# Both output projections of a two-layer encoder as seven products of halves, with weight sums built by adding DMAs

## The chip, the cores and the metric

The kernel runs on one core of a Trainium2 chip. The metric is the device time in microseconds of one execution. A difference is read from the median of several runs; the profile comes from one execution, whose time is given beside its span.

## The reference

A trunk of two encoder layers over 1024 tokens of width 1024, all float32. Each layer normalises, modulates by the conditioning vector, mixes tokens, and adds the mixer's output through an output projection and a gate:

```python
mod = c_act @ ada_w[layer] + ada_b[layer]
shift, scale, gate = jnp.split(mod, 3, axis=-1)
h = rms_norm(x, norm_w[layer]) * (1.0 + scale[:, None, :]) + shift[:, None, :]
...
return jnp.concatenate([oa, ob], axis=-1) @ w_out      # layer 0
...
return (oc * jax.nn.silu(gc)) @ w_out                  # layer 1
...
x = x + gate[:, None, :] * y
...
return rms_norm(x, final_norm)
```

Layer 0 mixes with two attention groups, layer 1 with windowed attention. Only the two products with `w_out` (1024 x 1024 each) and what surrounds them are changed.

## The kernel before

Everything is kept transposed: 128 partitions hold features, the free dimension holds tokens. A float32 matmul is made of three (`mm3`): each operand is split into a high part, rounded to the fast format, and a low part, the rest; high by high, high by low and low by high are added in PSUM. So each operand costs a cast and a subtraction ahead of its use. Tiles of 128 x 1024 come from one pool of 49 (`U`, `UR`), accumulators from eight PSUM banks of 128 x 512.

The kernel isn't issued as it is written. A recorder takes down every operation, a list scheduler gives each a start, and `emit` writes them out in that order; so all instructions carry the line of `emit` (L483 in the profile, L548 in the changed kernel), and groups are told apart by the names of tiles. On each engine instructions then run strictly in that order. Marks (`b703`, `("w", 3, 6)`, `("op", half, ft)`) name points in the program after which a load may be issued.

An output projection (`load_wo`, `load_oT`, `out_proj`) runs twice per layer, for tokens 0 to 511 and 512 to 1023. For each of eight output tiles `ft` and eight contraction steps `kc`, `mm3` multiplies a 128 x 128 block of weights (`wo0h`, `wo0l`; `wo1h`, `wo1l`) with 512 tokens of the mixer's output (`oTh`, `oTl`). In layer 1 the second half is done in two blocks of 256 tokens, so that the last block's end is short. DVE's scalar_tensor_tensor evacuates: residual plus gate column (`gcol`) times PSUM, in place in the residual (`xr`, `x1r`). Behind it ACT squares the new residual and POOL or DVE adds the squares (`sq`); when a half is complete, PE transposes the sums, DVE reduces them (`ss`), POOL takes the power (`r`), PE transposes `r` back, and the rows are normalised: in layer 0 for layer 1's input (`hT10`, `hT11`), in layer 1 for the output. `ada_at(("op", half, ft))` hangs the computation of layer 1's modulation columns (DVE operations on tiles `ada` and `adag`, four per place) on output tiles of layer 0's projection. Loads run on SP's queue; POOL's queue issues only sixteen small copies (`q<-qr_sp`).

## Time and profile before

| | |
|---|---|
| median of 3 runs | 1194.38 us (1193.34 to 1195.65) |
| profiled execution | 1192.36 us |
| its span, first to last instruction | 1190.6 us |
| mean granted TensorE clock | 0.995 |
| layer 0's projection, first and last start of a matmul with wo0h | 651.5 and 741.5 us |
| layer 1's, with wo1h | 1074.3 and 1179.9 us |

An engine's busy time is a union over the stretch; the chain of work that ended last is followed back from the last instruction, so an engine that fills the chain sets the end. A line group gives the busy time, the mean duration of one instruction, and the idle time in front with what ended it. Matmuls are pipelined: the duration of one is longer than the distance to the next, and only the distance is paid.

### The profile page before, as it was taken

Reading aid. Unit: us, or ns where it says so; the run is one execution under the profiler, and the core shown is the slowest. Engines: PE = TensorE matmul, PEld = TensorE weight load, DVE = VectorE, ACT = ScalarE, POOL = GpSimd, SP = SyncE. Lnnn points to the kernel's source line nnn. Section 1 sums busy time; section 2 is a strip of 40 time slices with the busy share of each in tenths; the row PEclk is TensorE's granted clock in tenths of the full one; section 3 lists DMA queues with packets and bytes.
Section 4 is the critical chain, followed back from the end, with each engine's and each line's share of the span. In section 5 each row is a group of like instructions: output and inputs, shape, how many; then the busy total and the mean of one; then the engine's idle time right before and its main releaser. Section 6 shows DMA issues by size and latency. Waiting matters only on the chain.

```text
span 1190.6 us, 17868 instructions
## 1 busy us (share of the span) xinstructions
PE 1161.9 (98%) x6320; PEld 982.7 (83%) x6320; DVE 904.8 (76%) x1693; ACT 657.1 (55%) x1371; POOL 581.1 (49%) x591
## 2 busy tenths in 40 slices
PE   8999999999999999999999999999999999999996
PEld 7898887878778778788778888988888888888896
DVE  7974678797777988888889984559886697788343
ACT  5653366566646867786868221328755545653212
POOL 1334496859456555453448324306456254467321
PEclk9999999999999999999999999999999999999999
DMA  9602212131112210101044664200012121055112
GB/s 370 246 1 79 99 40 72 54 124 36 51 62 89 89 53 19 36 18 36 2 160 164 246 243 159 72 1 19 19 54 74 36 88 54 18 198 178 68 72 71
DMA packets 33353, 106.18 MB, mean 89 GB/s; under 512 B 3696, under 2 KB 6256, under 8 KB 33264
## 3 DMA queue, kind: packets, MB, share of 16 engines
q1 hardware_dynamic: 32496, 102.96, 24.1%
q0 software_dynamic: 768, 2.10, 0.7%
q8 instruction: 49, 0.80, 0.3%
q14 instruction: 40, 0.33, 0.1%
HBM read 82.36 MB, written 22.68 MB: 88 GB/s over the span
## 4 chain that ended last, share of the span: by engine, by line
PE 84%; DVE 6%; ACT 4%; DMA 3%; issue 1%; POOL 1%; SPq 0%; POOLq 0%; DVEq 0%; ACTq 0%
PE psum L483 84%; DVE nm L483 2%; DMA ada<-in_ada_t 2%; DVE p L483 1%; DMA w2s<-in_w_c 1%; DMA w31s<-in_w_c 1%; ACT k L483 1%; ACT q L483 1%; ACT Pa L483 0%; DVE hla L483 0%; ACT p L483 0%; DVE hl L483 0%; DVE q L483 0%; DVE hlb L483 0%; POOL r L483 0%
## 5 line engine op out<-in xcount | busy, mean ns | idle before, releaser
L483 DVE TENSOR_REDUCE nm<-psum 128x1 f32<-128x1024 f32 x128 | 154.7, 1217 | 24.6 <-PE psum L483 23.0
L483 POOL TENSOR_SCALAR p<-p,dn 128x384 f32<-128x384 f32 (+1 forms) x128 | 74.1, 597 | 160.2 <-DVE dn L483 79.2
L483 DVE TENSOR_TENSOR hla<-psum,hla 128x512 fp32r<-128x512 f32 x128 | 84.3, 683 | 18.4 <-ACT hla L483 17.2
L483 PE MATMUL psum<-hla,VA 128*128 128x512 f32 x256 | 93.9, 425 | 3.7 <-DVE hla L483 3.5
L483 POOL TENSOR_SCALAR Pb<-Pb,rs 128x1024 f32<-128x1024 f32 x64 | 71.8, 1124 | 45.6 <-DVE rs L483 43.9
L483 ACT CAST hla<-psum 128x512 fp32r<-128x512 f32 x128 | 71.5, 597 | 40.3 <-PE psum L483 37.1
L483 PE MATMUL psum<-ident,Pa 128*128 128x128 f32 x512 | 91.6, 273 | 1.4 <-DVE q L483 0.8
L483 PE MATMUL psum<-hlb,VB 128*128 128x512 f32 x256 | 90.7, 427 | 2.1 <-DVE hlb L483 1.4
L483 POOL TENSOR_SCALAR Pa<-Pa,rs 128x1024 f32<-128x1024 f32 x64 | 73.6, 1154 | 39.2 <-DVE rs L483 37.0
L483 ACT ACTIVATE Pa<-psum,nm 128x1024 f32<-128x1024 f32 x64 | 71.7, 1121 | 35.7 <-DVE nm L483 31.5
L483 DVE TENSOR_TENSOR hlb<-psum,hlb 128x512 fp32r<-128x512 f32 x128 | 82.2, 683 | 7.7 <-ACT hlb L483 6.9
L483 ACT ACTIVATE Pb<-psum,nm 128x1024 f32<-128x1024 f32 x64 | 71.8, 1123 | 25.2 <-DVE nm L483 22.2
L483 PE MATMUL psum<-k,q 128*128 128x512 f32 x256 | 84.1, 399 | 0.2 <-ACT Pb L483 0.2
L483 DVE CUSTOM_DVE_ANT_0 p<-psum,bias,rows_g 128x384 f32<-128x384 f32 (+1 forms) x128 | 70.5, 578 | 12.8 <-PE psum L483 11.7
L483 PE MATMUL psum<-ident,Pb 128*128 128x128 f32 x512 | 79.4, 272 | 0.0
L483 ACT ACTIVATE p<-p,nm 128x384 f32<-128x384 f32 (+1 forms) x128 | 74.1, 585 | 7.1 <-DVE nm L483 7.1
L483 PEld LDWEIGHTS psum<-ident,Pa 128*128 128x128 f32 x512 | 64.3, 140 | 12.9 <-DVE gT L483 1.6
L483 ACT COPY ot<-psum 64x512 f32<-64x512 f32 x64 | 37.4, 584 | 67.5 <-PE psum L483 67.0
L483 ACT CAST hlb<-psum 128x512 fp32r<-128x512 f32 x128 | 68.9, 603 | 9.1 <-PE psum L483 7.8
L483 PEld LDWEIGHTS psum<-ident,Pb 128*128 128x128 f32 x512 | 63.1, 140 | 11.3
L483 POOL TENSOR_TENSOR sq<-sq,sq 128x256 f32<-128x256 f32 (+2 forms) x22 | 27.6, 1254 | 78.2 <-ACT sq L483 77.9
L483 PE MATMUL psum<-oTl,wo1h 128*128 128x256 f32 (+1 forms) x192 | 61.1, 319 | 0.0
(750 smaller groups left out, 3647.5 us busy)
## 6 DMA issues: line engine op xcount, KB each, us to landing
ada<-in_ada_t SPq DMA_DIRECT2D x32, 512.0 KB, 8.6
adag<-in_ada_t SPq DMA_DIRECT2D x16, 512.0 KB, 4.9
o<-spill SPq DMA_DIRECT2D x12, 512.0 KB, 5.6
xT<-in_xt SPq DMA_DIRECT2D x8, 512.0 KB, 8.2
wo0s<-in_w_out SPq DMA_DIRECT2D x8, 512.0 KB, 8.1
xr<-in_xt SPq DMA_DIRECT2D x8, 512.0 KB, 10.8
x_sp<-xr SPq DMA_DIRECT2D x8, 512.0 KB, 3.0
wo1s<-in_w_out SPq DMA_DIRECT2D x8, 512.0 KB, 5.7
```

The lines of the kernel that those rows point to most:

```text
L483: fn(*[real(v) for v in a], **{k: real(v) for k, v in kw.items()})
```

## The change

`wino_out` takes the place of `load_oT`, `load_wo`, `out_proj` and the layers' loops, in both layers. Weights and activations are cut into 2 x 2 halves (A11 to A22 by halves of the output and of the contraction features, B11 to B22 by halves of the contraction features and tokens). Instead of eight half products, seven are formed, in the order of phases "1", "2", "6", "7", "4", "5", "3". Each has four output tiles `u`, four steps `k` and three matmuls, with 512 tokens; phase 3 of layer 1 is done in two blocks of 256.

- Sums of weights: S1 = A21 + A22, S2 = A11 + A21 + A22, S3 = A11 + A21, S4 = A12 + A11 + A21 + A22, two tiles each. SP loads the first term, POOL's queue issues DMAs with `accum_op=add` for the others: 14 of 512 KB per layer.
- Combinations of activations T1 to T4: additions in place on POOL (T1, T4) and DVE (T3, T2).
- Splits: 14 weight tiles and 14 activation tiles a layer, high parts on ACT, low parts on DVE, or on POOL where `LO_POOL` says so (layer 0: A22 and S4).
- Results: phase 1's four accumulators are copied to SBUF by ACT (`sa`) and go on in PSUM into phase 2; `sa` is subtracted in place in phase 6's PSUM on DVE. A product that belongs to two outputs is added to both: 24 evacuations and 4 subtractions a layer in place of 16 evacuations. `ngcol` is the negated gate.
- Layer 1's second half keeps its residual in order of token blocks (`y_of`), its first block's last multiplications go to POOL and DVE, and its output leaves from ACT's queue.
- `ADA_AT` moves 16 operations `ada` of layer 1 from layer 0's projection to the preparation and the first places of the attention, and the gate's operations to other places.
- DRAM tiles are tracked by address range instead of by name, and `banks_in` assigns PSUM banks along the final order. `MOVES` is empty.

```diff
+LO_POOL = ((0, 0, 1, 0, 1), (0, 0, 0, 0, 0))
+T_POOL = (((0, 0), (0, 0), (1, 1), (1, 1)), ((0, 0), (0, 0), (1, 1), (1, 1)))
+L0_AT = (("b603"), ("b613"), ("b703"), ("b711"))
...
-ADA_AT = (8, 5, ("op", 0, 0), ("op", 0, 2), ("op", 0, 4), ("op", 0, 7), ("op", 1, 7), ("w", 2, 2))
+ADA_AT = (8, 5, ("c2", 6), 2, 4, 10, ("op", 1, 7), ("w", 2, 2))
...
-    def load_oT(l, half, kept, mark):
...
-    def load_wo(l, w, mark):
...
-    def out_proj(l, wo, oT, res, half, blocks, after, mark):
...
+    def y_of(l, half, res, ft, c0=0, n=512):
+        if (l, half) != (1, 1):
+            return chunk(res, ft)[:, c0:c0 + n]
+        t = res[ft // 2].rearrange("p (b e c) -> p b e c", b=2, e=2)
+        return t[:, :, ft % 2, :] if n == 512 else t[:, c0 // 256, ft % 2, :]
+    def like(y, t):
+        return t if len(y.shape) == 2 else t.rearrange("p (b c) -> p b c", b=2)
...
+            with rec.at(shift=0 if last or half == 0 else 300):
+                for k2 in (0, 1, 2, 3) if half == 0 else (2, 3, 0, 1):
+                    a, b = out[half, k2], res[k2]
+                    if n < 512:
+                        a = a.rearrange("p (e c) -> p e c", e=2)[:, :, c0:c0 + n]
+                        b = b.rearrange("p (b e c) -> p b e c", b=2, e=2)[:, c0 // 256]
+                    if last or half == 1 and k2 > 1:
+                        r_ = pr if last else rb
+                        (nc.vector if last else nc.gpsimd).tensor_tensor(
+                            out=b, in0=b, in1=r_.unsqueeze(1).broadcast_to([P, 2, n]), op=ALU.mult)
+                    else:
+                        for e in range(2):
+                            y = y_of(1, half, res, 2 * k2 + e, c0, n)
+                            nc.vector.scalar_tensor_tensor(out=y, in0=y, scalar=fn(2 * k2 + e), in1=rb if half == 0 else pr,
+                                                           op0=ALU.mult, op1=ALU.mult)
+                    (nc.sync if last or half == 0 else nc.scalar).dma_start(out=a, in_=b)
...
+        def comb(eng, o, a, b, op):
+            for o_, a_, b_ in each(o, a, b):
+                eng.tensor_tensor(out=o_, in0=a_, in1=b_, op=op)
+            return o
...
+        def split(ts, name, sign=1, lo_eng=None):
+            res_ = []
+            for j, t in enumerate(ts):
+                h, lo = [[x, x[:, 0:512], x[:, 512:1024]] for x in (UR(f"{name}h{j}"), UR(f"{name}l{j}"))]
+                for t_, h_ in each(t, h):
+                    if sign > 0:
+                        nc.scalar.copy(h_, t_)
+                    else:
+                        nc.scalar.activation(h_, t_, AF.Copy, scale=-1.0)
+                for t_, h_, l_ in each(t, h, lo):
+                    if sign > 0:
+                        (lo_eng or nc.vector).tensor_tensor(out=l_, in0=t_, in1=f(h_), op=ALU.subtract)
+                    else:
+                        nc.vector.scalar_tensor_tensor(out=l_, in0=t_, scalar=-1.0, in1=f(h_), op0=ALU.mult,
+                                                       op1=ALU.subtract)
+                res_ += [(h[1], lo[1]), (h[2], lo[2])]
+            return res_
...
+        def product(ps, A, B, u, first, c0=0, n=512):
+            for k in range(4):
+                m_ = mm3(ps[:, c0:c0 + n], [a[:, u * P:(u + 1) * P] for a in A[k]], [b[:, c0:c0 + n] for b in B[k]],
+                         first and k == 0, k == 3, skip_group_check=True)
...
+        def add_y(half, ft, ps, sign, c0=0, n=512):
+            y = y_of(l, half, res[half], ft, c0, n)
+            g = (gcol if sign > 0 else ngcol)[:, 8 * l + ft:8 * l + ft + 1]
+            nc.vector.scalar_tensor_tensor(out=y, in0=like(y, ps[:, c0:c0 + n]), scalar=g, in1=y, op0=ALU.mult, op1=ALU.add)
...
+        def sum_w(name, blocks_, mark):
+            ts = []
+            for j in range(2):
+                t = tile2(f"{name}{l}{j}")
+                for q, (b_, k) in enumerate(blocks_):
+                    if q == 0:
+                        load(t[0], w[b_, 2 * k + j], mark)
+                    else:
+                        behind(nc.gpsimd.dma_start(out=t[0], in_=w[b_, 2 * k + j], accum_op=ALU.add), mark)
+                ts.append(t)
+            return ts
...
+        A11, A12, A21, A22 = (0, 0), (0, 1), (1, 0), (1, 1)
+        res = [[U(f"xr{l}{half}{k2}") for k2 in range(4)] for half in range(2)]
+        B11 = [raw_o(0, k2, m[0]) for k2 in (0, 1)]
+        a11, b11 = split(sum_w("A11", [A11], m[0]), f"a11{l}"), split(B11, f"b11{l}")
+        for half in range(2):
+            for k2 in range(4):
+                if (l, half) == (1, 1):
+                    for e in range(2):
+                        load(res[half][k2].rearrange("p (b e c) -> p e b c", b=2, e=2)[:, e],
+                             res_src[half, k2].rearrange("p (e b c) -> p e b c", b=2, e=2)[:, e], m[1])
+                else:
+                    load(res[half][k2], res_src[half, k2], m[1])
+        B12 = [raw_o(1, k2, m[1]) for k2 in (0, 1)]
+        T1 = [comb(TE[2][j], tile2(f"t1{l}{j}"), B12[j], B11[j], ALU.subtract) for j in range(2)]
+        a = [PA(f"wa{l}{u}") for u in range(4)]
+        sa = [U(f"sa{l}{j}") for j in range(2)]
+        sa = [sa[u // 2][:, (u % 2) * 512:(u % 2 + 1) * 512] for u in range(4)]
+        def r1(u):
+            nc.scalar.copy(sa[u], a[u])
+        phase("1", a11, b11, a, True, r1)
+        B21 = [raw_o(0, k2, m[2]) for k2 in (2, 3)]
+        a12, b21 = split(sum_w("A12", [A12], m[2]), f"a12{l}"), split(B21, f"b21{l}")
+        s2 = split(sum_w("S2", [A11, A21, A22], m[2]), f"s2{l}", lo_eng=LO[0])
+        B22 = [raw_o(1, k2, m[k2]) for k2 in (2, 3)]
+        T3 = [comb(TE[0][j], B12[j], B12[j], B22[j], ALU.subtract) for j in range(2)]
+        T2 = [comb(TE[1][j], B11[j], B11[j], T3[j], ALU.subtract) for j in range(2)]
+        def r2(u):
+            add_y(0, u, a[u], 1)
+            after(0, u, 0, 512, u, res[0], False)
+        phase("2", a12, b21, a, False, r2)
+        t2 = split(T2, f"t2{l}")
+        T4 = [comb(TE[3][j], B21[j], B21[j], T2[j], ALU.subtract) for j in range(2)]
+        b = [PA(f"wb{l}{u}") for u in range(4)]
+        def r6(u):
+            nc.vector.tensor_tensor(out=b[u], in0=b[u], in1=sa[u], op=ALU.subtract)
+            add_y(1, u, b[u], -1)
+        phase("6", s2, t2, b, True, r6)
+        s3, t3 = split(sum_w("S3", [A11, A21], m[3]), f"s3{l}", lo_eng=LO[1]), split(T3, f"t3{l}")
+        phase("7", s3, t3, b, False, lambda u: add_y(1, 4 + u, b[u], 1))
+        a22, t4 = split(sum_w("A22", [A22], marks["wino", l, "6", 0]), f"a22{l}", lo_eng=LO[2]), split(T4, f"t4{l}")
+        def r4(u):
+            add_y(0, 4 + u, b[u], 1)
+            after(0, 4 + u, 0, 512, 4 + u, res[0], False)
+        phase("4", a22, t4, b, False, r4)
+        s1, t1 = split(sum_w("S1", [A21, A22], marks["wino", l, "7", 0]), f"s1{l}", lo_eng=LO[3]), split(T1, f"t1{l}")
+        c = [PA(f"wc{l}{u}") for u in range(4)]
+        def r5(u):
+            add_y(1, 4 + u, c[u], 1)
+            after(1, 4 + u, 0, 512, u, res[1], False)
+        phase("5", s1, t1, c, True, r5)
+        s4 = split(sum_w("S4", [A12, A11, A21, A22], marks["wino", l, "4", 0]), f"s4{l}", lo_eng=LO[4])
+        b22 = split(B22, f"b22{l}", sign=-1)
+        blocks = [(0, 512)] if l == 0 else [(0, 256), (256, 256)]
+        for c0, n in blocks:
+            def r3(u):
+                add_y(1, u, c[u], -1, c0, n)
+                after(1, u, c0, n, 4 + u, res[1], c0 + n == 512)
+            phase("3", s4, b22, c, False, r3, c0, n)
+        return res
...
-    wo0 = [load_wo(0, w_out0[0], marks["b703"]), None]
-    oT = load_oT(0, 0, kept0, marks["b703"])
-    res = load_res(xt[0], "xr0", marks["b703"])
-    wo0[1] = load_wo(0, w_out0[1], marks["b703"])
-    layer0_out(0, oT, res, None)
-    oT = load_oT(0, 1, kept0, marks["op", 0, 0, 2])
-    res = load_res(xt[1], "xr1", marks["op", 0, 0, 4])
-    layer0_out(1, oT, res, None)
...
+    wino_out(0, w_out0, kept0, L0_AT, xt, layer0_after())
...
-    wo1 = [load_wo(1, w_out1[0], marks["w", 3, 6]), None]
-    oT = load_oT(1, 0, keep, marks["w", 3, 5])
-    res = load_res(x1_sp[0], "x1r0", marks["w", 3, 6])
-    wo1[1] = load_wo(1, w_out1[1], marks["w", 3, 6])
-    layer1_out(0, oT, res, [(0, 512)])
-    oT = load_oT(1, 1, keep, marks["op", 1, 0, 1])
-    res = load_res(x1_sp[1], "x1r1", marks["op", 1, 0, 2])
-    layer1_out(1, oT, res, [(0, 256), (256, 256)])
...
+    wino_out(1, w_out1, keep, [("w", 3, 3), ("w", 3, 4), ("w", 3, 5), ("w", 3, 6)], x1_sp, layer1_after())
```

On POOL at the end of layer 0's first token half, before: `sq` sums squares of the residual, `oTl` are low parts of the mixer's output, `r` is the power for the half's norm.

```order
L483 TENSOR_TENSOR oTl_1277<-o_1278,oTh_1276 128x512 [waits PE_49,DMAHW7_49,Activation_49,Pool_49]
L483 TENSOR_TENSOR oTl_1280<-o_1281,oTh_1279 128x512 [waits DMAHW1_49,DVE_49,Activation_49]
L483 TENSOR_TENSOR sq_1245<-sq_1245,sq_1254 128x1024 [waits DMASW1_49,DMASW0_49,Activation_49]
L483 TENSOR_TENSOR oTl_1283<-o_1284,oTh_1282 128x512 [waits DVE_49,DMAHW6_49,Activation_49,Pool_49]
L483 TENSOR_TENSOR sq_1245<-sq_1245,sq_1259 128x1024 [waits Activation_49,Pool_49]
L483 TENSOR_TENSOR sq_1245<-sq_1245 128x512 [waits Pool_49]
L483 TENSOR_TENSOR r<-ss,mhalf 128x4 [waits DVE_49]
```

Nothing but these sums, low parts and the power stood here. In the changed kernel the same place, phases 6 to 5 of layer 0: S_1319 and S_1320 are the two tiles of S4, `s40l` their low parts, and `sq` and `r` as before.

```order
L548 DMA S_1319<-in_w_out 128x1024 [waits DMAHW1_49,PE_49]
L548 DMA S_1320<-in_w_out 128x1024 [waits DMAHW2_49,DVE_49]
L548 DMA S_1319<-in_w_out 128x1024 [waits DMASW2_49,DMASW0_49]
L548 TENSOR_TENSOR sq_1268<-sq_1268,sq_1294 128x1024 [waits Activation_49]
L548 DMA S_1319<-in_w_out 128x1024 [waits DMASW2_49]
L548 TENSOR_TENSOR sq_1268<-sq_1268 128x512 [waits Pool_49]
L548 DMA S_1320<-in_w_out 128x1024 [waits DMASW4_49,DMASW1_49]
L548 TENSOR_TENSOR s40l_1322<-S_1319,s40h_1321 128x1024 [waits DMASW3_49,DVE_49,Activation_49]
L548 TENSOR_TENSOR r<-ss,mhalf 128x4 [waits DVE_49]
L548 DMA S_1320<-in_w_out 128x1024 [waits DMASW4_49]
L548 TENSOR_TENSOR s40l_1324<-S_1320,s40h_1323 128x1024 [waits DMASW5_49,PE_49,Activation_49]
```

S4's adding DMAs now stand between the additions of squares, and `r` stands behind a low part that waits for the third DMA of the first tile; the third DMA of the second tile stands behind `r`.

On PE in the changed kernel, in the third output tile of phase 5 (activations t10, weights s10):

```order
L548 MATMUL psum<-t10h_1313,s10h_1309 128x512 [waits DVE_49]
L548 MATMUL psum<-t10l_1314,s10h_1309 128x512
L548 MATMUL psum<-t10h_1313,s10l_1310 128x512
L548 MATMUL psum<-ident,r 128x128 [waits Pool_49]
L548 MATMUL psum<-ident,r 128x128 x3
```

The transposes of `r` stand inside phase 5 and wait for POOL. The start of phase 3 on PE, behind the rest of phase 5 (b220 are the activations, s40 the weights of S4):

```order
L548 MATMUL psum<-b220h_1325,s40h_1321 128x512 [waits Activation_49]
L548 MATMUL psum<-b220l_1326,s40h_1321 128x512
L548 MATMUL psum<-b220h_1325,s40l_1322 128x512
L548 MATMUL psum<-b220h_1325,s40h_1321 128x512
L548 MATMUL psum<-b220l_1326,s40h_1321 128x512
L548 MATMUL psum<-b220h_1325,s40l_1322 128x512
L548 MATMUL psum<-b220h_1327,s40h_1323 128x512 [waits Activation_49]
L548 MATMUL psum<-b220l_1328,s40h_1323 128x512
L548 MATMUL psum<-b220h_1327,s40l_1324 128x512 [waits Pool_49]
```

It waits for the casts on ACT (s40h) and for POOL's second low part (s40l_1324); before, PE went on here with plainly loaded weights.

On POOL in layer 1, S2's four adding DMAs (tiles S_1753 and S_1754) stand in a row, and S3's (S_1768) behind them:

```order
L548 DMA S_1753<-in_w_out 128x1024 [waits DMAHW0_49]
L548 DMA S_1754<-in_w_out 128x1024 [waits DMAHW1_49,DMASW7_49,Pool_49]
L548 DMA S_1753<-in_w_out 128x1024 [waits DMASW6_49]
L548 DMA S_1754<-in_w_out 128x1024 [waits DMASW7_49]
L548 DMA S_1768<-in_w_out 128x1024 [waits DMAHW3_49,PE_49]
```

Before, POOL's queue had no DMAs here. On DVE their low parts `s21l`, combinations of activations (`o`), the last gate (`g`) and the low parts t21l and b211l follow each other:

```order
L548 TENSOR_TENSOR s21l_1756<-S_1753,s21h_1755 128x1024 [waits DMASW0_49,PE_49,Activation_49]
L548 TENSOR_TENSOR o_1736<-o_1736,o_1759 128x1024 [waits DMAHW2_49]
L548 TENSOR_TENSOR o_1724<-o_1724,o_1736 128x1024 [waits DVE_49]
L548 TENSOR_TENSOR s21l_1758<-S_1754,s21h_1757 128x1024 [waits DMASW1_49,PE_49,Activation_49]
L548 SCALAR_TENSOR_TENSOR g_1704<-g_1704,psum 128x512 [waits Activation_49]
L548 TENSOR_TENSOR t21l_1765<-o_1724,t21h_1764 128x1024 [waits DVE_49,PE_49]
L548 TENSOR_TENSOR s31l_1771<-S_1768,s31h_1770 128x1024 [waits DMASW2_49,PE_49,Activation_49]
L548 TENSOR_TENSOR o_1737<-o_1737,og_1635 128x512 [waits Pool_49]
L548 TENSOR_TENSOR b211l_1752<-og_1635,b211h_1751 128x512 [waits Activation_49]
```

Each second DMA waits for the first of its tile, and behind DVE's two low parts of S2 are queued t21l and b211l, which phases 6 and 2 read; before, DVE had low parts of plainly loaded weights (`wo1l`) and of the mixer's output (`oTl`) here.

More of the change, by code (lines that the diff above doesn't have):

```diff
@@ L479, in emit @@
         real = lambda v: v.real() if isinstance(v, VP) else v
+        seq = self.moved([o.i for o in sorted(self.ops, key=lambda o: (o.start, o.i))], MOVES)
+        self.banks_in(seq)
         with self.tc.manual_schedule():
[L481 removed]
+            for o in (self.ops[i] for i in seq):
                 fn, a, kw = o.call
@@ L1501, in encoder_kernel @@
+            hT1[half] = alloc_hT(1, half)
+            for kc in range(KC):
+                modulate(1, kc, chunk(res, kc), rb, hT1[half][kc], MOD_WAY[1][kc % len(MOD_WAY[1])])
+        return after
+    kept0 = {7: ogs["0", 7]}
+    wino_out(0, w_out0, kept0, L0_AT, xt, layer0_after())
     wv1 = wload([w_v1[j] for j in range(2)], 256, "wv1", mark=marks["op", 0, 1, 3])
```

228 lines of the change are left out of this document (138 added, 90 removed).

## Prediction

> **What bounds the kernel now.** I read the profile page first (busy time, then the chain that ended last), then the chain in order of time, then the table of windows for the two stretches that the change touches.
>
> ```profile
> PE 1161.9 (98%) x6320; PEld 982.7 (83%) x6320; DVE 904.8 (76%) x1693; ACT 657.1 (55%) x1371; POOL 581.1 (49%) x591
> ...
> PE 84%; DVE 6%; ACT 4%; DMA 3%; issue 1%; POOL 1%; SPq 0%; POOLq 0%; DVEq 0%; ACTq 0%
> ...
> 600.38 202.78 PE psum L483 x1059
> ...
> 1064.28 113.25 PE psum L483 x687
> ...
> core 0: us, PE busy (x) PEld busy (x) DVE busy (x) ACT busy (x) POOL busy (x), PEclk, DMA share, GB/s
> ...
> 651.00:742.00 91.00, 91.00 (x407) 75.20 (x406) 71.63 (x94) 20.85 (x31) 32.91 (x18) 1.00 0.61 223
> ...
> 1089.00:1181.00 92.00, 91.62 (x592) 83.76 (x590) 41.49 (x59) 21.51 (x43) 30.00 (x26) 1.00 0.18 64
> ```
>
> TensorE is busy for 98% of the span. In both projections the chain is one unbroken piece of PE work, at the full granted clock (1.00): there a matmul taken away is worth its issue time, as long as whatever replaces it is ready in time.
>
> ```profile
> L483 PE MATMUL psum<-oTl,wo0h 128*128 128x512 f32 x128 | 50.0, 390 | 0.0
> ...
> L483 PE MATMUL psum<-oTl,wo1h 128*128 128x256 f32 x128 | 36.4, 284 | 0.0
> ...
> L483 PE MATMUL psum<-oTl,wo1h 128*128 128x512 f32 x64 | 24.8, 389 | 0.0
> ...
> 699.70 0.39 PE L483 MATMUL psum<-oTh,wo0h 128*128 128x512 f32 x1
> ...
> 701.06 0.39 PE L483 MATMUL psum<-oTh,wo0h 128*128 128x512 f32 x1
> 701.29 0.60 PE L483 MATMUL psum<-ident,sq 128*128 128x128 f32 x4
> 701.64 0.48 PE L483 MATMUL psum<-oTl,wo0h 128*128 128x512 f32 x1
> ...
> 1177.00 0.28 PE L483 MATMUL psum<-oTh,wo1h 128*128 128x256 f32 x1
> ...
> 1177.96 0.28 PE L483 MATMUL psum<-oTh,wo1l 128*128 128x256 f32 x1
> ```
>
> The mean of 390 ns is a latency; the pipeline issues faster. Six matmuls lie between the starts 699.70 and 701.06: 0.227 us each for N = 512. Eight lie between 1177.00 and 1177.96: 0.120 us each for N = 256. Four transposes take 0.35 us of the queue (701.29 to 701.64). Each of the three kinds (high by high, high by low, low by high) has the counts shown, so layer 0 has 384 matmuls of N = 512; layer 1 has 192 of N = 512 and 384 of N = 256.
>
> **What is removed.** Seven products of 4 output tiles x 4 contraction steps x 3 are 336 matmuls a layer. Layer 0: 48 fewer, 48 x 0.227 = 10.9 us. Layer 1: six products at N = 512 (288) and the last one in two blocks of 256 (96): before 192 x 0.227 + 384 x 0.120 = 89.7 us, after 288 x 0.227 + 96 x 0.120 = 76.9, so 12.8 us. Together **23.7 us**, if PE never waits for the new operands.
>
> **What the sums of weights cost.** Each of the 28 accumulating DMAs waits for the one before it on its tile, so a sum is a chain. Its unit is L, the time from issue on POOL to landing of 512 KB added into SBUF. No row shows one.
>
> ```profile
> q<-qr_sp POOLq DMA_DIRECT2D x16, 128.0 KB, 2.8
> ...
> wukv<-in_w_ukv SPq DMA_DIRECT2D x1, 512.0 KB, 3.4
> ...
> wo0s<-in_w_out SPq DMA_DIRECT2D x8, 512.0 KB, 8.1
> ...
> xr<-in_xt SPq DMA_DIRECT2D x8, 512.0 KB, 10.8
> ...
> L483 POOL TENSOR_TENSOR sq<-sq,sq 128x1024 f32<-128x1024 f32 x4 | 10.7, 2670 | 37.3 <-ACT sq L483 37.3
> ...
> L483 POOL TENSOR_TENSOR r<-ss,mhalf 128x4 f32<-128x4 f32 x2 | 2.1, 1030 | 16.4 <-DVE ss L483 16.4
> ...
> L483 DVE SCALAR_TENSOR_TENSOR xr<-psum,gcol,xr 128x512 f32<-128x512 f32 x16 | 11.9, 744 | 16.9 <-PE psum L483 16.9
> L483 DVE TENSOR_TENSOR wo0l<-wo0s,wo0h 128x1024 fp32r<-128x1024 f32 x8 | 10.9, 1397 | 0.0
> ...
> L483 ACT ACTIVATE sq<-xr 128x1024 f32<-128x1024 f32 x6 | 6.4, 1063 | 36.1 <-DVE xr L483 36.1
> ```
>
> From below, 2.8 (POOL's own queue, a quarter of the bytes) and 3.4 (one plain load alone); from above 8.1 and 10.8, loads that stand in bursts behind others. The sums are spread over the phases rather than issued in a burst, so I go near the lower rows: 3.4 and about 1 us for software issue and the second operand, **L = 4.5**.
>
> The Trainium skill, "DMA: Bandwidth & Descriptors", section "Anatomy of one DMA", fits a software DMA as 2.0 us plus bytes over 436 GB/s; for 512 KB that gives an estimate of 3.2, and for the row of 128 KB 2.3 where the trace has 2.8. The Trainium skill, "Collectives: The Full Stack", section "The bandwidth ceiling", says that an adding transfer reads two sources and so halves the rate; doubling the data part gives an estimate of 4.4, and this rule speaks against the change. No run here shows an adding DMA yet; by 3.2 the stall of layer 0 below would be 0.5 us, by 4.4 it would be 2.7.
>
> Layer 0, sum S4 (last phase, "3"), counted from the start of phase 4. Output tile 1 ends after 24 x 0.227 = 5.4; its evacuation is 0.74, its square on ACT 1.06, the addition on POOL 2.67: 9.9. Only then comes the third adding DMA of the first tile in POOL's queue (order above), which lands at 9.9 + L. ACT's cast (same size as the 1.06) and POOL's low part (2.67) end at 13.7 + L, and behind them stands `r`, the 1/rms power of half 0 (1.03): 14.7 + L. PE's transposes of `r` come after 75 matmuls and four transposes, at 17.4, so PE waits L - 2.7. The second tile's last DMA is queued behind `r`: it lands at 14.7 + 2L, its cast and low part end at 18.4 + 2L, and PE wants them after 105 matmuls and eight transposes, at 24.5. The longer wait counts: **2L - 6.1** in all, 2.9 at L = 4.5. Behind PE's waits stands phase 3, and nothing else covers it.
>
> Layer 1, sum S2: between the attention output that POOL's queue waits for and the first matmul with t21l stand 109 PE rows, 24.7 us at the spacings above; POOL's two rows ahead (2 x 2.67) and ACT and DVE (1.3) leave 18. The chain is 2L, then in DVE's order a cast, two low parts, two combinations, one gate and t21l: 1.06 + 5 x 1.4 + 0.74 = 8.8. Stall 2L - 9, 0 at 4.5. Sum S4 of layer 1: the second tile lands at 9 + 2L after the start of phase 4, plus 3.5 for cast, DVE queue and low part, wanted at 24: 2L - 11.5, 0 at 4.5. Layer 0's S2 is issued a phase early and S1, S3 have one addition: 0 below L = 10.
>
> ```profile
> 678.98 2.40 POOL L483 TENSOR_TENSOR sq<-sq,sq 128x1024 f32<-128x1024 f32 x1 [13.98 <-ACT sq L483]
> ...
> 689.74 3.48 POOL L483 TENSOR_TENSOR sq<-sq,sq 128x1024 f32<-128x1024 f32 x1 [6.13 <-ACT sq L483]
> ```
>
> The same POOL addition took 2.40 or 3.48. If all three on layer 0's chain took 3.48, that adds 3 x 0.8 = 2.4 us.
>
> The Trainium skill, "SBUF — State Buffer", section "Who interferes with whom", states that a DVE instruction with two SBUF inputs contends with GpSimd reads. The spread of these two rows fits it but doesn't show the partner; by that rule DVE's many low parts would make 3.48 the price, and the sum would be 2.4 us more.
>
> **What is moved.** Sixteen DVE operations that prepare layer 1's modulation leave layer 0's output stage for the first attention:
>
> ```profile
> L483 DVE CUSTOM_DVE_ANT_0 ada<-ada,cb,a 128x1024 f32<-128x1024 f32 x8 | 12.9, 1607 | 0.0
> ...
> L483 DVE CUSTOM_DVE_ANT_0 ada<-ada,cb,cols 128x1024 f32<-128x1024 f32 x8 | 10.2, 1272 | 0.0
> ...
> 100.00:200.00 100.00, 99.46 (x553) 82.98 (x552) 65.62 (x98) 52.05 (x103) 59.99 (x58) 1.00 0.23 80
> 200.00:300.00 100.00, 97.83 (x519) 79.46 (x518) 80.60 (x127) 60.16 (x110) 77.96 (x76) 1.00 0.19 64
> ```
>
> That is 23.1 us into windows where DVE is idle for 34 and 19 us. Each can sit 1.3 to 1.6 us in front of a score maximum that PE needs soon; bounds are 0 and 23, and I take **1.5**, since PE loses only 2.7 us in these 200 us with DVE already at 73%. The four new in-place subtractions, 8 more evacuations a layer (0.74 each), the negated gate column and the copies of phase 1 lie on DVE and ACT under PE. Layer 1's final block is 256 tokens as before: the tail after the last matmul stays.
>
> ```profile
> 1180.12 0.28 PE L483 MATMUL psum<-oTh,wo1l 128*128 128x256 f32 x1
> ...
> 1183.96 2.48 DVE L483 TENSOR_TENSOR x1r<-x1r,psum 128x512 f32<-128x512 f32 x4 [1.38 <-PE psum L483]
> 1184.68 2.56 SPq L483 DMA_DIRECT2D out<-x1r  x4
> ```
>
> From 1180.12 to the end of the span (1190.6) are 10.5 us; the block of 256 before it goes out on POOL and ACT's queue earlier, bounds -1 to +1, value 0.
>
> **Sum.** Profiled execution 1192.36 (span 1190.6): - 23.7 + 2.9 + 1.5 = 1173.1. The runs' median, 1194.38, is 2.0 above that execution, so the forecast is **1175 us**.
>
> **Rivals.**
> - Everything is hidden (L up to 3, no cost in the attention): 1192.4 - 23.7 + 2.0 = 1171. For it: the rows of 2.8 and 3.4, and PE's clean chain. Against it: the second DMA chain behind `r`. The fit in the Trainium skill's "DMA: Bandwidth & Descriptors", "Anatomy of one DMA", nearly gives this time by its estimate of 3.2.
> - VectorE becomes the bound of the projection.
>
> ```profile
> L483 DVE SCALAR_TENSOR_TENSOR psum<-xr,mods,psum 128x512 f32<-128x512 f32 x16 | 11.1, 748 | 0.9 <-PE psum L483 0.9
> ...
> L483 DVE TENSOR_TENSOR oTl<-o,oTh 128x512 fp32r<-128x512 f32 x8 | 6.8, 873 | 0.0
> ...
> L483 DVE SCALAR_TENSOR_TENSOR hT10l<-psum,mods,hT10h 128x512 fp32r<-128x512 f32 x8 | 5.5, 741 | 0.0
> ```
>
>   In layer 0 it gets 28 operations from PSUM (28 x 0.74 = 20.7), ten weight low parts (14.0), 28 half low parts of activations at 0.87 (24.5), four combinations (5.6) and the modulation of both halves (11.1 and 16 x 0.74 = 11.9): 88 us, against 336 x 0.227 = 76 of PE plus the lead of the first phase. The windows show 71.6 in 91 before, with 23 of that moved away. If a tenth of it (9 us) shows: 1184. Against it: part of the splits falls before the stage.
> - Slow adding DMAs eat the gain. The three stalls sum to 6L - 26.6; with 1.5 they reach 23.7 at **L = 8.1**, just the row of wo0s. At 10.8, the row of xr: 15.5 + 12.6 + 10.1 = 38.2, so 1192.4 - 23.7 + 38.2 + 1.5 + 2.0 = **1210**, slower than before. Place: PE's waits for s40l and for t21l. Against it: the loads with 8 to 11 us stand in bursts of eight.
> - The change might not drop the matmuls it says: the loops give 336 a layer, so 6320 - 48 - 192 = 6080 in all; I give this no chance.
>
> **How the numbers follow.** Forecast (L about 3.4 to 6.5, 1172 to 1182): 0.45. All hidden: 0.22. VectorE as bound, 1182 to 1190: 0.18. Slow DMAs: 0.15, of which 0.04 near no change and 0.11 slower. The range runs from 1168 (all hidden, 3 us better from the tail and the attention) to 1192. A measurement can tell about 0.2% from no change: faster 0.85, same 0.04, slower 0.11.
>
> **What would show it.** Right: 6080 matmuls; PE busy down by about 24 us; POOL's issues of the S tiles landing in 4 to 5 us; PE waits of about 2 and 1 us for `r` and for s40l in layer 0, none in layer 1. Wrong: landing times of 8 us and more, waits of PE for t21l or s41l, DVE without idle time in the output stages with PE waiting for low parts, or PE waits for `nm` grown in the first attention.

## The result, and the profile after

| | before | changed |
|---|---|---|
| median of 4 runs each, same chip | 1195.02 us | 1210.16 us |
| lowest and highest | 1193.34, 1197.37 | 1209.47, 1210.67 |
| span of the profiled execution | 1190.6 us | 1208.0 us |
| mean granted TensorE clock | 0.995 | 0.982 |

The ratio is 1.0125, with a 95% interval of 1.0106 to 1.0144: the changed kernel is slower by 1.25%. The forecast was 1175, with a range from 1168 to 1192.

The page of the changed kernel, first the busy time, then the chain that ended last by engine, then its landing times of DMAs:

```profile
PE 1153.2 (95%) x6080; PEld 966.0 (80%) x6080; DVE 954.7 (79%) x1743; ACT 699.4 (58%) x1405; POOL 613.3 (51%) x604
...
PE 68%; DMA 10%; DVE 9%; ACT 5%; issue 4%; POOL 3%; SPq 0%; POOLq 0%; DVEq 0%; ACTq 0%
...
S<-in_w_out POOLq DMA_DIRECT2D x28, 512.0 KB, 8.1
```

The 240 matmuls are gone (6320 to 6080), but PE's busy time fell only from 1161.9 to 1153.2, and its idle time rose from 28.7 (1190.6 - 1161.9) to 54.8. DMA has 10% of the chain where it had 3%; by the page 7% are DMAs into the tiles `S`, in which the sums are built. Half of the adding DMAs land within 8.1 us.

The waits of PE in the two projections of the changed kernel (total, times, longest; the first six rows are 640 to 760 us, the others 1085 to 1208):

```profile
PE psum L548 <- ACT s40h L548: 3.8, 1, 3.8
PE psum L548 <- DVE xr L548: 3.1, 1, 3.1
PE psum L548 <- POOL r L548: 2.0, 1, 2.0
PE psum L548 <- POOL s40l L548: 1.2, 1, 1.2
...
PE psum L548 <- DVE s20l L548: 0.6, 1, 0.6
PE psum L548 <- DVE sq L548: 0.6, 1, 0.6
...
PE psum L548 <- DVE g L548: 7.2, 1, 7.2
PE psum L548 <- ACT rbz L548: 3.4, 1, 3.4
...
PE psum L548 <- DVE t21l L548: 0.3, 1, 0.3
```

These sum to 22.2 us, and none of them is there in the kernel before. The rows left out here are waits that the run without sums, below, has too (0.4 to 1.8 us each). Five names (`xr`, `r`, `sq`, `g`, `rbz`, together 16.3) aren't tiles of weights: on DVE, ACT and POOL they are queued behind an operation that waits for a sum, or need one that is.

The second loss is in the matmuls themselves. The windows of the changed kernel (length, busy time of PE, PEld, DVE, ACT, POOL, then the granted clock):

```profile
651.00:742.00 91.00, 81.43 (x351) 65.32 (x349) 64.16 (x75) 36.58 (x47) 36.29 (x26) 0.94 0.79 204
685.00:690.00 5.00, 2.24 (x5) 1.82 (x6) 5.00 (x6) 2.19 (x3) 1.12 (x1) 0.71 0.55 205
690.00:695.00 5.00, 5.00 (x15) 3.90 (x14) 3.05 (x4) 2.10 (x2) 3.38 (x2) 0.61 0.89 307
...
1130.00:1135.00 5.00, 5.00 (x14) 3.91 (x14) 5.00 (x4) 4.53 (x6) 1.88 (x1) 0.58 0.00 0
```

Before, the clock was 1.00 in both projections. Here the windows of 5 us show 0.5 to 0.7 behind each longer wait, as the timeline of PE shows at 687.76:

```profile
687.76 0.79 PE L548 MATMUL psum<-t20h,s20h 128*128 128x512 f32 x1 [3.06 <-DVE xr L548]
688.35 0.63 PE L548 MATMUL psum<-t20l,s20h 128*128 128x512 f32 x1
688.78 0.63 PE L548 MATMUL psum<-t20h,s20l 128*128 128x512 f32 x1
689.20 0.63 PE L548 MATMUL psum<-t20h,s20h 128*128 128x512 f32 x1
```

The starts are 0.427 us apart instead of 0.227. Taking windows of 5 us over the span and adding up PE busy time times (1 - clock), the loss is 13.4 us, against 2.6 in the kernel before; 10.7 of it lie in the two projections. (These windows mix slow and full stretches and count a little low: by the five stretches at half clock themselves the projections lose 11.6.)

How long an adding DMA takes depends on its neighbours. The rows are the landing times of the POOL-issued tiles `S` in four stretches of the changed kernel: two that follow each other, each with another beside it for at most 3.5 us (713 to 721 us), two that start 2 us apart beside loads of the same stage (658 to 662), one beside loads of the next stage (730 to 731), and five at the end (1155 to 1173), each of which overlaps the one before or behind it:

```profile
S<-in_w_out POOLq DMA_DIRECT2D x2, 512.0 KB, 5.4
...
S<-in_w_out POOLq DMA_DIRECT2D x2, 512.0 KB, 9.8
...
S<-in_w_out POOLq DMA_DIRECT2D x1, 512.0 KB, 11.1
...
S<-in_w_out POOLq DMA_DIRECT2D x5, 512.0 KB, 5.6
```

So L is 5.3 to 5.6 at best, and about 10 where the two tiles of a sum are built side by side while plain loads are in flight too. Three that overlapped each other with no load beside them (669 to 681) took 7.1, 7.9 and 9.1. How much of the 10 is the partner's and how much the loads' was not separated.

### The profile page after: what moved, and what is told of

Same layout as the page of the kernel before. It is cut to its first block, busy times and chain, and to the rows that moved or that the text cites. A ratio compares the mean times of both kernels' runs of the same rounds, so it can differ in the third digit from the quotient of the medians.

```text
span 1208.0 us, 17544 instructions
## 1 busy us (share of the span) xinstructions
PE 1153.2 (95%) x6080; PEld 966.0 (80%) x6080; DVE 954.7 (79%) x1743; ACT 699.4 (58%) x1405; POOL 613.3 (51%) x604
## 4 chain that ended last, share of the span: by engine, by line
PE 68%; DMA 10%; DVE 9%; ACT 5%; issue 4%; POOL 3%; SPq 0%; POOLq 0%; DVEq 0%; ACTq 0%
PE psum L548 68%; DMA S<-in_w_out 7%; DVE nm L548 2%; DMA ada<-in_ada_t 2%; DVE p L548 1%; POOL sq L548 1%; DMA w2s<-in_w_c 1%; ACT Pa L548 1%; DMA w31s<-in_w_c 1%; ACT k L548 1%; ACT q L548 1%; DVE hla L548 1%; DVE xr L548 1%; DVE hl L548 0%; ACT p L548 0%
## 5 line engine op out<-in xcount | busy, mean ns | idle before, releaser
L548 POOL TENSOR_SCALAR Pa<-Pa,rs 128x1024 f32<-128x1024 f32 x64 | 78.8, 1238 | 41.7 <-DVE rs L548 38.3
L548 DVE TENSOR_TENSOR hla<-psum,hla 128x512 fp32r<-128x512 f32 x128 | 83.7, 681 | 10.5 <-ACT hla L548 9.8
L548 DVE CUSTOM_DVE_ANT_0 p<-psum,bias,rows_g 128x384 f32<-128x384 f32 (+1 forms) x128 | 70.5, 578 | 12.2 <-PE psum L548 10.8
L548 PEld LDWEIGHTS psum<-ident,Pa 128*128 128x128 f32 x512 | 64.3, 141 | 11.7 <-DVE q L548 1.0
L548 PEld LDWEIGHTS psum<-hla,VA 128*128 128x128 f32 x256 | 46.9, 192 | 20.1 <-DVE hla L548 8.8
L548 ACT CAST hl<-psum 128x512 fp32r<-128x512 f32 x88 | 46.5, 593 | 28.0 <-PE psum L548 22.0
```

The costliest lines, as they stand in the source:

```text
L548: fn(*[real(v) for v in a], **{k: real(v) for k, v in kw.items()})
```

## The experiments

"Changed" is 1210.16. Each run has the kernel before beside it on the same chip, in parentheses; ratios are to that, with 95% intervals.

### The sums left out

```diff
+                if "accum_op" in kw:
+                    continue
```

The 28 adding DMAs aren't issued; the sums keep their first terms alone, and the order is otherwise the same.

> The 28 adding DMAs are left out, so each sum of weights holds its first term alone; every other instruction stays in its place in the order. Theory A (PE waits in the projections because adding DMAs land 8 to 11 us after issue and ACT, DVE and POOL queue behind them): the waits for the sums go (3.8 + 3.1 + 2.0 + 1.2 + 0.6 in layer 0, 7.2 + 3.4 in layer 1) and with them the stretches at a granted clock of 0.5 to 0.7 behind them, about 10 us: 1210 falls to 1175 to 1182. Rival B (VectorE and ScalarE are the bound, with 14 + 14 splits a layer): the time stays above 1195 and PE goes on waiting for low parts.

Measured: 1174.40 (1195.33), ratio 0.9823 [0.9808, 0.9837]. The page:

```profile
span 1172.7 us, 17484 instructions
...
PE 1138.9 (97%) x6080; PEld 957.5 (82%) x6080; DVE 956.8 (82%) x1743; ACT 699.4 (60%) x1405; POOL 593.0 (51%) x576
```

All waits listed above are gone, and DVE does the same work (956.8 against 954.7) without holding PE up. So the sums cost 35.8 us, more than the whole loss of 15.1; VectorE isn't the bound. PE's idle time is 33.8, 21.0 less than in the changed kernel; the clock loss, by the same windows of 5 us, is 1.7, or 11.7 less: together 32.7 of the 35.3 us between the two spans.

### The same traffic without adding, and adding half of it

```diff
+                if "accum_op" in kw:
+                    kw = {k: v for k, v in kw.items() if k != "accum_op"}
```

The same 28 DMAs, as plain copies: each overwrites its tile.

> The same 28 DMAs from POOL's queue, same bytes and order, but as plain copies that overwrite instead of adding (so the sums are wrong: each holds its last term). Theory A1 (it is the addition that is slow: two operands per byte): landing falls from 5.5 alone and 8 to 11 in pairs to 3 to 5, and the time to 1178 to 1190. Rival A2 (it is the software queue, or the traffic of the other loads): landing stays at 8 and the time at 1203 to 1210.

Measured: 1187.63 (1195.33), ratio 0.9936 [0.9918, 0.9954]. They land after 5.4 us in the middle (3 to 5 was expected), against 8.1, and POOL issues one in 0.53 us where an adding one took 0.87. Adding, its longer issue included, is 22.5 us of the 35.8; the other 13.2 are there with plain copies in the same chains.

```diff
+                if "accum_op" in kw:
+                    kw = {**kw, "out": kw["out"][:, 0:512], "in_": kw["in_"][:, 0:512]}
```

Adding DMAs on the first 512 columns of each tile alone; the other columns keep the first term.

> The 28 adding DMAs in their places, each with the first 512 of 1024 columns only (the second half of each sum holds its first term). Theory (an adding DMA's landing is a fixed part of about 2 us plus bytes at some 140 KB per us, shared by all that are in flight): alone 5.5 becomes 3.7, pairs 8 to 11 become 4.5 to 6, and the time falls to 1178 to 1188. Rival (landing is set by POOL's software or by the chain of semaphores, not by bytes): landing and time stay, 1205 to 1210.

Measured: 1191.37 (1195.43), ratio 0.9958 [0.9942, 0.9974]; slower than expected. The page says why:

```profile
S<-in_w_out POOLq DMA_DIRECT2D x28, 256.0 KB, 5.4
```

With the least beside them, half the bytes took 3.9 to 4.1 us instead of 5.3 to 5.6, but with others in flight still up to 9.0, where the whole took up to 11.1. Halving the bytes takes away a quarter of the shortest landings, not half.

### Only S4 left out

```diff
+                if "accum_op" in kw and any(x.startswith("S4") for x in o.tiles):
+                    continue
```

The 12 adding DMAs of S4 aren't issued.

> Only S4's 12 adding DMAs are left out (S4 holds A12 alone), the other 16 stay. By the waits of the profile: S4 caused r 2.0, s40h 3.8, s40l 1.2 in layer 0 and rbz 3.4 in layer 1, with two of the stretches at a lower clock, about 15 of the 36 us: 1193 to 1197. Rival (every sum counts by its bytes, 12 of 28): 15 of 36 as well by bytes, but then S2's waits for g (7.2) and xr (3.1) shrink too because traffic is gone, 1185 to 1190.

Measured: 1191.17 (1195.43), ratio 0.9971 [0.9958, 0.9984]. S4 accounts for 19.0 us, more than expected; the waits for `xr` (3.1) and `g` (7.0) stay, so the sums that are left, by these waits S2 above all, make the other 16.8.

### Two parts of the change on the kernel before

Only the new `ADA_AT`, that is the sixteen `ada` operations moved into the first attention:

> The kernel before with only the places of layer 1's modulation moved as in the change. Theory: the 16 operations cost the first attention 2.7 us (the shift of its last matmul with hla between the two profiles), and the projection before has room for them anyway: 1197 to 1199. Rival: they are free, 1195, and the 2.7 us come from something else.

Measured: 1196.86 (1195.33), ratio 1.0014 [1.0001, 1.0027]: 1.5 us by the medians, just below what was expected, with an interval of 0.1 to 3.2; it agrees with the forecast's 1.5 for that term.

Only layer 1's last residuals in blocks of tokens (`y_of`, the multiplications of the first block on POOL, the output on ACT's queue):

> The kernel before with only the layout of layer 1's last residuals by blocks of tokens, the first block's multiplications on POOL and DVE and its output from ScalarE's queue. Theory (the tail behind the last matmul is 10.5 us in the kernel before and 11.0 in the changed one, so this part changes nothing): 1194 to 1196.5. Rival: the block before last costs PE waits or lengthens the tail, 1197 or more.

Measured: 1196.84 (1194.41), ratio 1.0018 [1.0002, 1.0035]: 0.2 to 4.2 us slower by itself, where nothing was forecast. Where these come from was not looked into. In the changed kernel the last matmul of a product starts at 1196.9 and the span ends at 1208.0, 11.1 us against 10.5, so there the blocks cost about half a microsecond at the end.

### Waits put into the kernel before

To see what a wait costs beyond its length, six waits were put into layer 0's projection of the kernel before: behind chosen output tiles ACT copies a PSUM tile 1, 2, 3, 4, 7 or 11 times, and a transpose of the result holds PE up.

```diff
+                x = U(f"gap{half}{ft}")
+                nc.scalar.copy(x[:, 0:512], ps)
+                for _ in range(copies):
+                    nc.scalar.copy(x[:, 0:512], x[:, 0:512])
+                pt = PA(f"gap{half}{ft}")
+                gap[0] = nc.tensor.transpose(out=pt[:, 0:P], in_=x[:, 0:P], identity=ident)
```

> The kernel before with six waits put into layer 0's projection: behind output tiles 0, 3, 6 of the first half and 1, 3, 5 of the second, a transpose on PE waits for 1, 2, 3, 4, 7 and 11 copies of 128x512 on ScalarE that read the finished tile; about 1.0, 1.5, 2.1, 2.6, 4.4 and 6.5 us. Theory (a wait of some 2 us or more halves the granted clock behind it, and each costs 2 to 3 us more than it lasts): matmul starts 0.43 us apart for 4 to 6 us behind the three or four long ones, 0.227 behind the short ones; 1195 + 18 + 8 to 12 = 1221 to 1226. Rival (the lower clock in the changed kernel comes from the traffic or from the whole load, not from the waits): starts stay 0.227 apart, 1213.

Measured: 1215.59 (1194.41), ratio 1.0178 [1.0151, 1.0205], between the two. PE's waits in 640 to 760 us, then the timeline behind the longest:

```profile
PE psum L484 <- ACT gap L484: 8.1, 4, 3.7
PE psum L484 <- DVE oTl L484: 3.1, 1, 3.1
PE psum L484 <- DVE hlb L484: 1.8, 1, 1.8
```

```profile
729.89 0.48 PE L484 MATMUL psum<-ident,gap 128*128 128x128 f32 x1 [3.70 <-ACT gap L484]
730.01 0.78 PE L484 MATMUL psum<-oTh,wo0h 128*128 128x512 f32 x1
730.59 0.63 PE L484 MATMUL psum<-oTl,wo0h 128*128 128x512 f32 x1
731.01 0.63 PE L484 MATMUL psum<-oTh,wo0l 128*128 128x512 f32 x1
```

With no adding DMA in the program, the same slow matmuls stand behind a wait. The waits of 1.7 and 1.8 us had none behind them; those of 2.0, 3.1 and 3.7 were followed by 3.4 to 5.2 us of them. The clock loss in this stage is 5.2 us for 13.0 of waits (some 18 had been planned, which is part of why the time came out below the theory's), so the slower clock is a consequence of waiting and needs no adding DMA. The whole clock loss of this execution is 11.3, 8.7 more than before; the 3.5 outside the stage lie ahead of it and have nothing to do with the waits that were put in.

### Later landings allowed for: the price, the marks, and both

The list scheduler that sets the order counts any POOL-issued DMA as 410 KB per us and 540 ns of issue, so it believed that a sum's 512 KB land in about 3 us. Three runs keep all 28 adding DMAs and change that price, the marks from which the sums may start, or both:

```diff
-            return 540, 0
+            return (870 if "accum_op" in kw else 540), 0
-                        dma_free = max(dma_free, t + 1300) + nb / 410.0
+                        dma_free = max(dma_free, t + 1300) + nb / (140.0 if "accum_op" in o.call[2] else 410.0)
...
-        s2 = split(sum_w("S2", [A11, A21, A22], m[2]), f"s2{l}", lo_eng=LO[0])
+        s2 = split(sum_w("S2", [A11, A21, A22], m[1]), f"s2{l}", lo_eng=LO[0])
-        s1, t1 = split(sum_w("S1", [A21, A22], marks["wino", l, "7", 0]), f"s1{l}", lo_eng=LO[3]), split(T1, f"t1{l}")
+        s1, t1 = split(sum_w("S1", [A21, A22], marks["wino", l, "6", 0]), f"s1{l}", lo_eng=LO[3]), split(T1, f"t1{l}")
-        s4 = split(sum_w("S4", [A12, A11, A21, A22], marks["wino", l, "4", 0]), f"s4{l}", lo_eng=LO[4])
+        s4 = split(sum_w("S4", [A12, A11, A21, A22], marks["wino", l, "7", 0]), f"s4{l}", lo_eng=LO[4])
```

Both:

> The change with all its adding DMAs, but the scheduler counts each at 140 KB per us in place of 410 and POOL's issue at 870 ns, and S2, S1 and S4 may be issued one phase earlier (S2 at the residual's mark, S1 from phase 6, S4 from phase 7). Theory that only the order around late sums costs, since the traffic itself fits: 1180 to 1192. Rival that adding traffic cannot be hidden wherever it stands (28 x 5 us = 140 us of the DMA engines beside the loads): 1200 or more.

The price alone (the first four lines):

> The changed kernel with the planner's price of an adding DMA alone (140 KB per us, 0.87 us of issue), its marks where they were: the same DMAs may start no earlier than before, but what stands behind them on TensorE, ACT, DVE and POOL is ordered for the later landing. Theory (the wait behind an in-order queue is most of the loss): the sums' cost of 35.8 us shrinks by a third to two thirds without any mark moved, 1186 to 1199 us, with the xr, g and rbz waits gone and those for s40h or s4l left. Rival (the sums are simply asked for too late, and only the earlier marks of the run planned for 5 us helped): 1203 to 1211 us, with waits of about the same total on other names.

The marks alone (the last six):

> The changed kernel with the earlier marks alone (S2 with the tiles of phase 1, S1 at phase 6, S4 at phase 7) and the planner's old price of an adding DMA (410 KB per us, 0.54 us). Theory (the sums are asked for too late; the order behind them is the smaller part): 1188 to 1195 us, S4's last adding DMA of layer 0 issued 10 us or more earlier than the 730.2 of the changed kernel, its waits for s40h, s40l and the first r nearly gone. Rival (both are needed, since with the old price the planner still puts the readers right behind the landing that it believes in): 1196 to 1206 us, with waits for s20h or s21h of several us in the places where S2 is used.

| | old marks | earlier marks |
|---|---|---|
| old price | 1210.16 | 1209.07 (1195.81), 1.0114 [1.0093, 1.0134] |
| new price | 1206.04 (1195.39), 1.0088 [1.0066, 1.0109] | 1188.54 (1195.43), 0.9949 [0.9930, 0.9968] |

Neither part does much alone (4.1 and 1.1 us), both together 21.6: my theory fell in each of the two single runs, and the marks alone did even less than the rival had it. With the price alone S4 still starts where its mark lets it (layer 0's last adding DMA is issued at 734.9, in the changed kernel at 730.2) and PE waits 4.8 us for `s40h` and 5.2 for `s20h`. With the marks alone it is issued at 715.2, and `s40h` and `s40l` hold PE up no longer; but PE stops for 10.7 us elsewhere. The timeline of that run, on ACT, POOL, DVE and PE in turn:

```profile
720.32 1.05 ACT L548 CAST s40h<-S 128x1024 fp32r<-128x1024 f32 x1 [15.60 <-DMA S<-in_w_out]
721.28 1.05 ACT L548 ACTIVATE sq<-xr 128x1024 f32<-128x1024 f32 x1
...
726.07 2.33 POOL L548 TENSOR_TENSOR s40l<-S,s40h 128x1024 fp32r<-128x1024 f32 x1
...
729.65 1.49 DVE L548 TENSOR_TENSOR sq<-sq,sq 128x512 f32<-128x512 f32 x2 [10.98 <-POOL sq L548]
...
731.28 1.09 PE L548 MATMUL psum<-ident,sq 128*128 128x128 f32 x4 [10.68 <-DVE sq L548]
```

Here the mechanism is bare. Asked for early, S4's cast was also put early in ACT's order, where by the old price its operand should have been there. It waits 15.6 us for the DMA, and the squares of the finished residual stand behind it; POOL's and DVE's additions wait for those, PE's transposes of `sq` for DVE, and behind the transposes stand matmuls whose operands had long been ready.

### The sums on VectorE

Every term is loaded plainly by SP, S1 is kept and reused (S2 = A11 + S1, S4 = S2 + A12), and DVE adds: eight additions a layer.

```diff
+        def plus(eng, o, x):
+            for j in range(2):
+                eng.tensor_tensor(out=o[j][0], in0=o[j][0], in1=x[j][0], op=ALU.add)
+            return o
...
+        S1 = raw_w("S1", *A21, m[2])
+        plus(SUM[l][0], S1, raw_w("S1x", *A22, m[2]))
+        S2 = plus(SUM[l][1], raw_w("S2", *A11, m[2]), S1)
```

> Same seven products, but the weights come by plain loads alone and the sums are made by 8 additions a layer on VectorE (S2 from S1, S4 from S2). Theory A: no chain of DMAs any more, about 10 us more work on VectorE a layer, 1175 to 1190 and below the kernel before. Rival B (VectorE is the bound): the added 20 us come on top, 1210 or more.

Measured: 1188.19 (1195.33), ratio 0.9944 [0.9927, 0.9961], within what was expected.

The same, with more low parts on POOL, `LO_POOL = ((0, 1, 1, 0, 1), (0, 1, 1, 1, 0))`:

> The plain loads and 8 additions a layer on VectorE as in e3, with the low parts of S3 (both layers) and of A22 and S1 (layer 1) on POOL, since e3 has PE waiting for t30l, t31l and xr behind VectorE, and POOL idle there. Theory (VectorE's queue is what is left): 1178 to 1185. Rival (POOL and VectorE share what they read and slow each other, 1.2 to 3.4 us for a low part): 1188 or more.

Measured: 1185.46 (1195.43), ratio 0.9922 [0.9903, 0.9941], half a microsecond above what was expected. Layer 0's waits on sums fall to 0.6 us; layer 1 keeps 2.6 for `t21h`, 1.9 for `t21l` and 3.1 for `r`.

As the first of these, but with layer 1's S3 by one adding DMA per tile (counted at 140 KB per us), where one landing has a phase of time:

> Seven products; sums on VectorE from plain loads as in e7, but layer 1's S3 by one adding DMA per tile, counted at 140 KB per us by the scheduler, and layer 1's low parts back on VectorE. Theory (in e7 what is left is layer 1's VectorE queue, where additions and low parts take 2.3 to 3.4 us in place of 1.2 while POOL works too): 1179 to 1184. Rival (the lone adding DMAs of 5.5 us are late again): 1187 or more.

Measured: 1182.82 (1194.41), ratio 0.9901 [0.9873, 0.9929]: 1.0% faster than the kernel before, and 2.2% faster than the changed one (0.9901 over 1.0125). PE's longest waits in its projections are 2.8 (`r`), 1.4 (`t30l`) and 1.2 us (`t31l`). It is some 8 us behind the run without any sums.

## Why the prediction was wrong

| term | forecast | measured |
|---|---|---|
| matmuls removed | -23.7 | PE busy 1161.9 to 1138.9 with the sums out: -23.0 |
| `ada` moved | +1.5 | +1.5 on the kernel before (0.1 to 3.2) |
| tail | 0 | about +0.5 in place; +2.4 by itself |
| layer 0, waits on S4 | +2.9 | 7.0 (3.8 + 2.0 + 1.2) |
| layer 0, waits behind S2 | 0 | 3.7 (`xr`, `s20l`); `sq` 0.6 besides |
| layer 1, waits behind S2 | 0 | 7.5 (`g`, `t21l`) |
| layer 1, waits behind S4 | 0 | 3.4 (`rbz`) |
| slower clock behind waits | not there | +10.7 |

**The removal, right.** The count is 6080, and without the sums the whole change comes to 20.9 us less (1195.33 to 1174.40): 23.7 less 1.5 leaves 1.3 for the tail and the rest.

**The step that failed** is the price of the sums: "The sums are spread over the phases rather than issued in a burst, so I go near the lower rows ... L = 4.5". The shortest landings are 5.3 to 5.6, the middle is 8.1. A sum is itself a small burst, two tiles issued together, and where loads were in flight beside such a pair it landed after 9 to 11 us; the last DMA of layer 0 met the next stage's loads and took 11.1. I had rows of 8.1 and 10.8 for loads behind others, and set them aside. The fit in the Trainium skill, "DMA: Bandwidth & Descriptors", section "Anatomy of one DMA", gave an estimate of 3.2; the traces have 5.3 at best for an adding DMA of 512 KB, and 3.7 at best for a plain copy from the same queue. The rule of two sources in the Trainium skill, "Collectives: The Full Stack", section "The bandwidth ceiling", gave 4.4, also too low, but its direction holds: adding is slower than copying by 22.5 us over the kernel.

**The chain, right for layer 0.** The critical chain of the changed kernel goes the way that was worked out: the third DMA of S4's first tile, `s40h`, `s40l`, `r`, the last DMA, the second `s40l`:

```profile
720.28 5.32 DMA S<-in_w_out
...
726.76 2.37 POOL s40l L548
729.13 1.02 POOL r L548
730.16 11.11 DMA S<-in_w_out
...
742.48 2.36 POOL s40l L548
```

The mechanism was right there and the size off: two landings of 16.4 us together in place of 9. With these two put into the prediction's own count (14.7 + 16.4 + 3.7 behind the start of phase 4, at 709.81), PE's matmul with the second low part is due at 744.6; it started at 744.88. The waits for S4 are 7.0 where the formula gives 10.3 for such landings; PE came to them later than counted, by 1.7 us of slower clock and the 0.6 us for `sq` among others.

**The places valued at 0, wrong.** "Layer 0's S2 is issued a phase early and S1, S3 have one addition: 0 below L = 10", and 2L - 9 and 2L - 11.5 for layer 1. The two landings in layer 1's chain of S2 took 9.6 and 8.9 us; with 18.5 for 2L, 2L - 9 gives 9.5, and the wait for `g` was 7.2. In the other two places the sum was followed to its own reader, but PE waited for work queued behind it. Layer 1's S4, on ACT and then PE:

```profile
1178.42 1.04 ACT L548 CAST s41h<-S 128x1024 fp32r<-128x1024 f32 x1 [1.87 <-DMA S<-in_w_out]
...
1180.00 0.56 ACT L548 COPY rbz<-psum 128x512 f32<-128x512 f32 x1
...
1180.62 0.50 PE L548 MATMUL psum<-t11h,s11h 128*128 128x512 f32 x1 [3.44 <-ACT rbz L548]
```

PE's matmul of phase 5 needs nothing of S4; it waits for a copy that stands behind S4's cast.

**A term that was missing:** the slower clock behind waits, 10.7 us. The prediction read the granted clock as 1.00 and let it stay so.

**The rival that came true** is that of slow adding DMAs, at its upper end (L = 10.8, 1210 us, slower, chance 0.11). That its number fits is in part luck (forecast 1175, plus 22.2 - 2.9 of waits, plus 10.7 of clock make 1205 of the 1210; the other 5 were not taken apart): it had 38.2 us of waits, where the trace has 22.2 of waits and 10.7 of clock. VectorE as the bound fell with the run without sums.

**Why the order was so tight** is answered by the table of price and marks: the sums were asked for too late for a landing of 5 to 11 us, and their readers were placed for one of 3 us. Traffic as such doesn't forbid the change: with both corrected, 28 adding DMAs run 0.5% faster than the kernel before. What the remaining 14.1 us to the run without sums consist of (1188.54 against 1174.40) was not taken apart further, nor the last 2.6 us of the 35.3.

## What to carry to other kernels

A transfer that stands in a chain has to be priced as it will run, with its own partner and the loads of that stage in flight, and where a scheduler sets the order that price and the point of asking must be corrected together: here each alone gained 1 to 4 us, both 22. On engines that run strictly in order, list what is queued behind an operation that waits for a DMA; three quarters of the waits here bore the names of bystanders. And once PE is made to wait for 2 us, count up to about 3 us more for the matmuls behind.

## What the runs showed of the hardware

- **Adding DMAs.** Of the 28 of 512 KB in the changed kernel, eight took 5.3 to 5.6 us from issue to landing; none of these shared more than its first 3.0 us with an earlier one from POOL's queue. The others took 6.2 to 11.1. Plain copies of the same size from the same queue took 3.7 to 8.0, and adding DMAs of 256 KB 3.9 to 9.0. Issue on POOL: 0.87 us against 0.53.
- **The clock.** In the two projections of the changed kernel each of the five waits of 2.0 us and more was followed by 3.4 to 6.1 us of PE work at 0.427 us per matmul instead of 0.227. The length of the wait alone doesn't decide: waits of 1.8 and 1.9 were followed by such a stretch in some executions and not in others, and with the price alone waits of 2.1 and 2.4 had none behind them. What does decide shows when all fifteen traces are cut along the clock's own steps. Within an execution the stretches at half clock begin on a grid of 3.41 us and last whole steps of it, but for the one that ends the execution. Of the steps at full clock, each of the 48 in which PE idled 1.95 us or more was followed by a step at half clock, and none of the 5040 with 1.55 or less; of the 33 between, 13 were. In the changed kernel a wait of 2.40 us that ended at 15.34 was split over two steps and cost nothing more; the one of 1.99 at 730.21 lay within one. The columns are as in the windows above, the clock the third from the end:

```profile
11.22:14.64 3.42, 1.71 (x16) 1.47 (x14) 3.15 (x7) 1.53 (x2) 1.48 (x1) 1.00 1.04 412
14.64:18.05 3.41, 2.71 (x24) 2.60 (x24) 2.99 (x5) 1.70 (x3) 0.64 (x1) 1.00 1.02 406
18.05:21.46 3.41, 3.41 (x18) 3.08 (x17) 3.41 (x5) 1.72 (x2) 0.00 (x0) 1.00 1.04 411
...
728.02:731.43 3.41, 1.42 (x9) 1.09 (x9) 0.84 (x2) 1.06 (x1) 3.05 (x3) 1.00 0.90 262
731.43:734.84 3.41, 3.41 (x10) 2.64 (x9) 3.41 (x6) 2.03 (x3) 0.00 (x0) 0.50 0.90 300
734.84:738.26 3.42, 3.42 (x17) 2.78 (x15) 2.08 (x4) 0.00 (x0) 0.00 (x0) 1.00 1.05 275
```

  The Trainium skill, "TensorE: Matmul & The Clock Gate", section "HAM oscillation — how this bites in real kernels", warns of idle gaps above about 3.4 us. By that rule the wait of 3.06 in the row of 687.76 should have cost nothing more, and the trace differs.
- **DVE beside POOL.** A subtraction of 128 x 1024 took 1.22 us on DVE at 712.29, where POOL computed nothing, and 4.26 at 673.42, where POOL issued a DMA and ran two additions in the same time. Not every overlap costs: the one at 1128.42 took 1.22 too, though POOL began an addition 0.17 us after it.

```profile
673.42 4.26 DVE L548 TENSOR_TENSOR t20l<-o,t20h 128x1024 fp32r<-128x1024 f32 x1
...
712.29 1.22 DVE L548 TENSOR_TENSOR s10l<-S,s10h 128x1024 fp32r<-128x1024 f32 x1 [0.34 <-ACT s10h L548]
...
1128.42 1.22 DVE L548 TENSOR_TENSOR t21l<-o,t21h 128x1024 fp32r<-128x1024 f32 x1
1128.59 3.29 POOL L548 TENSOR_TENSOR og<-og,g 128x1024 f32<-128x1024 f32 x1 [2.41 <-DVE g L548]
```
